# Gate weights split ahead of their stage, w2's last units in other buffers, and a second plain block at the start of FFN-b

## The chip, the cores and the metric

The kernel runs on one core of one Trainium2 chip. The metric is device microseconds of one execution. Its engines are called here by the profile's names: PE is TensorE (PEld its weight loads), DVE is VectorE, ACT is ScalarE, POOL is GpSimd, SP is SyncE, which issues nearly all transfers of this kernel.

## What is computed

One layer of a decoder trunk, for 1024 prompt rows and 32 sample rows that share the weights. They are handled together as 1056 columns.

```python
def swiglu(x, w1, w3, w2):
    return (jax.nn.silu(x @ w1) * (x @ w3)) @ w2

h = layer_norm(ALPHA * x + 0.5 * swiglu(x, f1_w1, f1_w3, f1_w2), ln1_g, ln1_b)      # FFN-a
z = h @ w_in + b_in                       # q, k, v, the gMLP's u and v, and two gates ga, gb
# att: dilated sliding-window attention on q, k, v;  yb: gMLP branch on u, v
mix = (jax.nn.sigmoid(ga) * (att @ w_oa) + jax.nn.sigmoid(gb) * (yb @ w_ob)) @ w_out
h = layer_norm(ALPHA * h + mix, ln2_g, ln2_b)
h = layer_norm(ALPHA * h + 0.5 * swiglu(h, f2_w1, f2_w3, f2_w2), ln3_g, ln3_b)      # FFN-b
```

D_MODEL is 1024, D_FF is 2816, so the hidden layer of an FFN is 22 blocks of 128 rows. All data is fp32.

## The kernel before

**Tiles.** Features lie on the 128 partitions, the 1056 columns in four chunks c = 0 to 3 of C = 264. Every fp32 operand is split into a high part (a cast to fp32r on ACT) and a low part (a subtraction on DVE), line 237, and every product is three matmuls of 128x128 by 128x264 (`mm3`, line 223): high by high, high by low, low by high. All of them carry line 227 in the profile.

**FFN** (`ffn`, line 641, called with i = 0 for FFN-a and i = 2 for FFN-b). The 22 hidden blocks are worked in two ways:

- `hidden8` (407) is the plain way: per chunk 8 x 3 matmuls for w3 and as many for w1, then Silu on ACT and a product on DVE. Block 0 is done so, chunk by chunk, while the chunks of the input become ready.
- `hidden` (424) is one level of Strassen over pairs of chunks and halves of the features: seven products of 2 x 4 x 3 matmuls each. `prep` (355) makes the sums of weights for it, a step per product of the block before; on DVE for the first two blocks, then on POOL. Its first two products need only chunks 0 and 2. `spread` (314) makes the sums of the input.

Blocks 0, 19, 20 and 21 (`PLAIN`) go as hidden rows to DRAM; the other 18, in pairs, go there as the sums that w2's Strassen needs (`spill_sums`, 459).

**The w2 stage** (`out`, 785). Three groups g of four blocks np run `seven` (762), with the sums loaded from DRAM ahead. In the last group `plain_sums` (798) reads the four plain blocks' hidden rows, splits them and writes both parts to DRAM (`parted`). In the last block, `fetch` loads them back (H, two slots each), and `units2` (757) loads w2's four units for the plain blocks, through a raw buffer each and a split. Then, per chunk, eight `block(n, c)` add the plain blocks' product, a unit for two n; two of the four units are taken in chunk 0, at n = 1 and 3 (line 898). `center` (518) subtracts the mean, with two DVE subtractions one step apart (line 537), `square_step` sums squares, and `norm` (582) makes the LayerNorm of a chunk: sums by PE (589), inverse root (`rsqrt`, 628: Sqrt on ACT, then four DVE operations), broadcast by PE (597), scaling on DVE (608) and ACT (616), and a split. Each chunk's LayerNorm runs beside the next work.

**After FFN-a** (`widen`, 1047): six of the sixteen gate blocks are multiplied the plain way (`gate8`, 948), the first three chunk by chunk while the LayerNorm ends, then three more (1077); then the Strassen pairs of w_in. Their weights are loaded by `unit` (212): a raw buffer, a cast, a subtraction. The first three are taken during w2's chunk 2 (line 892). The attention and the rest of the layer follow (`mix`, 1488). It ends with w_out and LayerNorm 2, whose last chunks overlap block 0 of FFN-b (673 to 683); block 0's weights are loaded at line 1626.

**Order and buffers.** The program order is what the code below writes; a scheduler then places each instruction by priority and by its own timeline, within each engine's order. `high_priority` moves a piece ahead; `fenced` and `chained` keep background pieces behind what was marked. Background work is written as generators in the queues `bg`, `slow` and `mid`, each stepped a few times after a product (`tick`, 179; the counts are in `STEPS`). `tables` (908) is such a piece, in FFN-a's w2 stage. On-chip buffers are taken from pools by tag: 37 slots S, 8 W, 2 raw R, 2 Q, 6 M. A transfer or an instruction that needs a buffer waits until one is free. `copy_state` (205) attaches pieces of a copy of state, DRAM to DRAM, to the loads of weights.

Of the kernel before, what the change touches and what calls it, by code (L numbers as in the profile page):

```python
# [13 lines left out]
F32R = mybir.dt.float32r  # L14
AF = mybir.ActivationFunctionType
# [49 lines left out]
WARM = 2  # L65
FENCED = (mybir.EngineType.DVE, mybir.EngineType.Activation, mybir.EngineType.SP)
# [5 lines left out]
EARLY = 6  # L72
CHUNKED = 3
# [6 lines left out]
class Trunk:  # L80
# [131 lines left out]
    def unit(self, src, n=D, slot=False, ahead=URGENT):  # L212
        new = self.S if slot else self.W
        with self.tc.high_priority(offset=ahead):
            raw = self.R([P, D])
            hi, lo = new([P, D], F32R), new([P, D], F32R)
            dma = self.nc.sync.dma_start(raw[:, :n], src[:, :n])
            self.split(hi[:, :n], lo[:, :n], raw[:, :n])
        self.fence[mybir.EngineType.SP] = dma.ins
        self.copy_state(dma, 1)  # L220
        return hi, lo
# [296 lines left out]
    def center(self, c, hs, rest, m=None, parts=1):  # L518
        nc = self.nc
        start = 0 if m is None else KB // 2 - 1  # L520
        t = self.M([P, C])
        y = self.Y[c]
        tt = nc.vector.tensor_tensor
        for i in range(start, KB // 2):
            m = self.gather(c, i, m)
            yield
        tt(t, m[:, 0], m[:, 1], op=ALU.add)
        tt(t, t, hs[:, c * C : c * C + C], op=ALU.add)
        yield from self.pause(rest)
        pm = self.ax_tile()[:, :C]  # L530
        nc.tensor.matmul(pm, self.ones, t, start=True, stop=True)
        yield from self.pause(rest if parts == 1 else 2)
        q = KH // parts
        for j in range(2):
            for x in range(0, KH, q):
                e = y[j][:, x : x + q]
                tt(e, e, pm.unsqueeze(1).to_broadcast([P, q, C]), op=ALU.subtract)
            yield
# [43 lines left out]
    def norm(self, c, i, mode, Y, s):  # L582
# [7 lines left out]
        r, t = self.X([P, 3], "rs"), self.X([P, 3], "rt")  # L590
        self.rsqrt(r, t, pv, EPL)
# [35 lines left out]

    def rsqrt(self, r, t, v, eps):
        tt = self.nc.vector.scalar_tensor_tensor
        self.nc.scalar.activation(r, v, AF.Sqrt, bias=self.eps[eps])  # L630
        self.nc.vector.reciprocal(r, r)
        tt(t, v, eps, r, op0=ALU.add, op1=ALU.mult)
        tt(t, t, -0.5, r, op0=ALU.mult, op1=ALU.mult)
        self.chain = tt(r, t, 1.5, r, op0=ALU.add, op1=ALU.mult).ins
# [6 lines left out]
    def ffn(self, w13, w2p, w2, i, mode, resid):  # L641
        nc, preps = self.nc, {}
        last = FB + NG * (KB // 2) - 1
# [27 lines left out]
        else:  # L671
# [17 lines left out]
        def ready(f):  # L689
            for _ in preps.pop(f):  # L690
                pass
            if f < last:
                begin(f + 1)

        def between(f, bg, slow=0):
            if f + 1 in preps:
                next(preps[f + 1], None)
            self.tick(bg, slow)
# [7 lines left out]
        for f in range(1, FB):  # L706
# [5 lines left out]
            def after():  # L712
# [4 lines left out]
            self.hidden(f, after)  # L717
            del self.L[f]
# [66 lines left out]
    def out(self, w2, i, mode, ready, between, load):  # L785
        nc = self.nc
        f = FB
        self.w2units, self.spare = self.units2(w2), False
# [4 lines left out]
        def fetch(k):  # L793

            if k < NPL:
                H.append(self.load_hidden(k))

# [33 lines left out]
        for g in range(NG):  # L831
            for np in range(KB // 2):
                final = g == NG - 1 and np == KB // 2 - 1
                if g == NG - 2 and np == 0:
# [9 lines left out]
                ready(f)  # L844

                def step(p):
# [26 lines left out]
        self.spare = True  # L873
# [13 lines left out]
        for c in range(NC):  # L887
            early = 6 if c == 0 else 0
            if mode != "out":
                self.hold_normed(c)  # L890
                if c == 2:
                    self.early = [self.unit(self.a["wzp"][n], slot=True, ahead=AFTER) for n in range(CHUNKED)]
            for n in range(KB):
# [4 lines left out]
                if c == 0 and n in (1, 3):  # L898
                    W2.append(next(self.w2units))
# [147 lines left out]
    def widen(self):  # L1047
# [585 lines left out]
    def run(self):  # L1633
# [8 lines left out]
        self.parted = parted("A")  # L1642
        self.ffn(a["w13a"], a["w2pa"], a["w2a"], 0, "spill", a["xc"])
# [150 lines left out]
```

## Time and profile before

| what | us |
|---|---|
| median of 3 runs | 2209.47 |
| lowest, highest | 2204.01, 2209.97 |
| the profiled execution's own time | 2205.9 |
| its span, first to last instruction | 2204.1 |

How to read the profile's lines. A line of a group or of the order of time names the engine, the line of the kernel, the operation, what it writes <- what it reads (buffer numbers left out), shapes, and xcount; in the order of time it begins with the start and the duration in us, and the bracket at its end is the idle time of the engine just before it and who ended it. SPq marks the issue of a transfer. A line of stretches is A:B and its length, then busy us and (xcount) of PE, PEld, DVE, ACT and POOL, the granted TensorE clock as a share of full speed, the mean busy share of the 16 DMA engines and GB/s. A line of one tile's operations gives the least, median and greatest duration in ns, first and last start in us, and the forms.

### The profile page before, as it was taken

The numbers are of one execution on the slowest core, as the hardware profiler recorded it, in microseconds if no ns is written. First come the engines' busy times: TensorE is split into PE (matmuls) and PEld (weight loads), VectorE is DVE, ScalarE is ACT, GpSimd is POOL, SyncE is SP. The second block draws the span as 40 slices with busy tenths as digits, with TensorE's granted clock in tenths as the row PEclk, the third lists the DMA queues.
The fourth block names the chain that finished last, engine by engine and source line by source line (L and its number), as shares of the span: only waits on it lengthen the run. The fifth ranks groups of instructions, "written<-read, shape, count | busy, mean of one in ns | idle before, by whom it ended". The sixth has DMA issues, their size and how long they took to land.

```text
span 2204.1 us, 43247 instructions
## 1 busy us (share of the span) xinstructions
PE 2148.7 (97%) x17281; PEld 2097.4 (95%) x17281; DVE 1560.7 (71%) x2718; ACT 899.0 (41%) x1690; POOL 327.2 (15%) x238
## 2 busy tenths in 40 slices
PE   9999999999999999999889998998999999999997
PEld 8999999999999999999878888998999999999997
DVE  8777777656788636888574648878676676657787
ACT  5444444421226634344365444246444444422224
POOL 0432332100010021322000000000432332100000
PEclk9999999999999999999989999999999999999999
DMA  4445545598874325666844647513445545597752
GB/s 157 146 142 178 169 160 190 182 381 315 337 269 145 121 102 190 222 213 243 289 155 147 186 133 236 202 44 132 165 156 176 175 160 181 186 381 268 294 191 79
DMA packets 170553, 429.82 MB, mean 195 GB/s; under 512 B 24864, under 2 KB 61456, under 8 KB 167664
## 3 DMA queue, kind: packets, MB, share of 16 engines
q1 hardware_dynamic: 169920, 426.53, 55.1%
q8 instruction: 135, 2.21, 0.4%
q10 hardware_dynamic: 432, 0.54, 0.1%
q14 instruction: 66, 0.54, 0.1%
HBM read 305.97 MB, written 167.22 MB: 215 GB/s over the span
## 4 chain that ended last, share of the span: by engine, by line
PE 84%; DMA 6%; DVE 6%; ACT 1%; issue 1%; POOL 1%; SPq 0%; ACTq 0%; DVEq 0%; POOLq 0%
PE ax L227 44%; PE mm L227 35%; DMA M<-kv 3%; PE ax L1164 1%; DVE W L239 1%; DMA R<-wz 1%; PE ax L1187 1%; PE ax L1203 1%; DMA S<-zD 1%; DVE S L239 1%; DVE S L608 1%; DMA S<-cD 0%; DMA R<-w2a 0%; DVE X L1346 0%; DVE M L1356 0%
## 5 line engine op out<-in xcount | busy, mean ns | idle before, releaser
L227 PE MATMUL ax<-S,W 128*128 128x264 f32 x5472 | 716.2, 285 | 0.8 <-ACT S L994 0.5
L227 PE MATMUL mm<-S,W 128*128 128x264 f32 x5040 | 676.8, 289 | 21.8 <-DVE S L1505 8.6
L227 PEld LDWEIGHTS ax<-S,W 128*128 128x128 f32 x5472 | 685.6, 188 | 3.4 <-ACT S L994 1.5
L227 PEld LDWEIGHTS mm<-S,W 128*128 128x128 f32 x5040 | 639.2, 190 | 37.9 <-DVE S L1505 8.9
L227 PE MATMUL ax<-S,S 128*128 128x264 f32 x3288 | 483.6, 285 | 3.1 <-DVE S L1003 3.0
L227 PEld LDWEIGHTS ax<-S,S 128*128 128x128 f32 x3288 | 434.1, 188 | 4.2 <-DVE S L1003 4.1
L227 PE MATMUL mm<-S,S 128*128 128x264 f32 x2496 | 390.3, 287 | 9.0 <-ACT S L238 4.5
L227 PEld LDWEIGHTS mm<-S,S 128*128 128x128 f32 x2496 | 339.8, 190 | 11.6 <-ACT S L238 4.9
L238 ACT CAST W<-R 128x256 fp32r<-128x256 f32 (+2 forms) x172 | 127.6, 759 | 323.6 <-PE mm L227 128.6
L369 POOL TENSOR_TENSOR Q<-R 128x512 f32<-128x512 f32 x50 | 70.7, 1415 | 793.9 <-DMA R<-w13b 240.2
L239 DVE TENSOR_TENSOR W<-R,W 128x256 fp32r<-128x256 f32 (+2 forms) x172 | 149.2, 872 | 27.1 <-ACT W L238 26.8
L238 ACT CAST W<-Q 128x1024 fp32r<-128x1024 f32 (+1 forms) x79 | 77.8, 985 | 216.5 <-POOL Q L370 89.8
L780 DVE SCALAR_TENSOR_TENSOR S<-ax,S 128x264 f32<-128x264 f32 x240 | 100.0, 432 | 69.1 <-PE ax L227 67.8
L444 DVE TENSOR_TENSOR S<-ax,M 128x264 f32<-128x264 f32 x84 | 33.7, 433 | 157.5 <-PE ax L227 157.5
L106 POOL CAST S<-ones 128x1 fp32r<-128x1 f32 x32 | 17.6, 571 | 752.5 <-DVE S L1583 366.5
L239 DVE TENSOR_TENSOR S<-Q,S 128x1024 fp32r<-128x1024 f32 (+1 forms) x79 | 114.0, 1443 | 3.4 <-ACT S L238 3.3
L239 DVE TENSOR_TENSOR W<-Q,W 128x1024 fp32r<-128x1024 f32 (+1 forms) x79 | 91.9, 1163 | 24.7 <-ACT W L238 24.7
L238 ACT CAST S<-Q 128x1024 fp32r<-128x1024 f32 (+1 forms) x79 | 77.8, 984 | 73.7 <-PE ax L227 54.6
L238 ACT CAST S<-R 128x512 fp32r<-128x512 f32 (+1 forms) x65 | 44.6, 686 | 110.7 <-DMA sumsA<-S 35.7
L239 DVE TENSOR_TENSOR S<-S,M 128x528 fp32r<-128x528 f32 x72 | 84.0, 1166 | 3.5 <-ACT M L238 1.9
L370 POOL TENSOR_TENSOR Q<-Q,R 128x512 f32<-128x512 f32 x50 | 83.4, 1668 | 2.7
L377 POOL TENSOR_TENSOR Q<-R,Q 128x512 f32<-128x512 f32 x50 | 81.7, 1634 | 1.2
(199 smaller groups left out, 2095.8 us busy)
## 6 DMA issues: line engine op xcount, KB each, us to landing
ws<-st SPq DMA_DIRECT2D x144, 256.0 KB
S<-sumsA SPq DMA_DIRECT2D x63, 528.0 KB
S<-sumsB SPq DMA_DIRECT2D x63, 528.0 KB
M<-kv SPq DMA_DIRECT2D x96, 256.0 KB
sumsA<-M SPq DMA_DIRECT2D x90, 264.0 KB
sumsB<-M SPq DMA_DIRECT2D x90, 264.0 KB
R<-w13b SPq DMA_DIRECT2D x44, 512.0 KB
S<-zD SPq DMA_DIRECT2D x42, 528.0 KB
```

The lines of the kernel that those rows point to most:

```text
L227: mm = lambda a, b, s, e: nc.tensor.matmul(o, a[:, cc], b, start=s, stop=e, skip_group_check=True)
L238: a = self.nc.scalar.copy(hi, src)
L239: b = self.nc.vector.tensor_tensor(lo, src, hi.bitcast(F32), op=ALU.subtract)
L369: tt(s12[:, lo], cd[:, lo], cd[:, hi], op=ALU.add)
L370: tt(s12[:, hi], s12[:, lo], ab[:, lo], op=ALU.subtract)
L377: tt(s34[:, hi], ab[:, hi], s12[:, hi], op=ALU.subtract)
L444: go(one, 5, False, lambda x: tt(h[:, x, 1], one[x], p7[:, x], op=ALU.add))
L608: nc.vector.tensor_tensor(y, y, pb.unsqueeze(1).to_broadcast([P, KH, C]), op=ALU.mult)
L780: nc.vector.scalar_tensor_tensor(y(x, r, e), bank[x], HALF, y(x, r, e), op0=ALU.mult, op1=ALU.add)
L1164: nc.tensor.matmul(pS[h][:, r, :nk], q[e, i * P : (i + 1) * P], k[e, k0 : k0 + nk], start=True, stop=True)
L1187: nc.tensor.transpose(pT[r][:, h, o], s[:, r, h, o], self.ident)
L1203: nc.tensor.matmul(pv[0][e, (i % 4) * P : (i % 4 + 1) * P], V[:, i - (nb - 1) + b, e], sT[:, r, h, b * P : b * P + P], start=b == 0, stop= ...
```

## The change

1. **Gates.** A new background piece, `part_gates`, starts with FFN-a's w2 stage. It loads the six gate blocks' weights in twelve halves, splits them and writes both parts to DRAM. `gate_unit` later loads the two parts straight into S slots (the first three) or W (the rest), where `unit` loaded one raw block and split it. In `widen`, the first Strassen pair's preparation is fenced and chained.
2. **w2's units, both FFNs.** All four are taken in the last block of the w2 stage, in an order with the fetches given by `FINAL` (0 is a unit, k is a fetch). Units three and four use the raw buffers Q, not R. No state copy is attached to them.
3. **Center.** In the w2 stage the two subtractions of chunks 1 to 3 are three steps apart, not one.
4. **FFN-b** begins with two plain blocks, 0 and 19, chunk by chunk in turn; block 19's Strassen form is dropped. The input's second `spread` enters the background before the last chunk.
5. **Inverse root on DVE** (`rsqrt_dve`): eleven DVE operations from a bit pattern and three Newton steps, in LayerNorm 2's last chunk and the last LayerNorm's chunk 2. After LayerNorm 2's chunk 2, ACT runs a small Silu.

```diff
+MAGIC = float(0x5F3759DF)
+FINAL = ((1, 0, 0), (0,), (2, 0), (3,))
...
-    def unit(self, src, n=D, slot=False, ahead=URGENT):
+    def unit(self, src, n=D, slot=False, ahead=URGENT, raw=None, copies=1):
...
-            raw = self.R([P, D])
+            raw = (raw or self.R)([P, D])
...
+    def part_gates(self):
+        nc = self.nc
+        halves = [(n, slice(e, e + D // 2)) for n in range(NLEAD) for e in (0, D // 2)]
+        raws = deque()
+
+        def start():
+            if todo:
+                n, e = todo.popleft()
+                raws.append(self.M([P, D // 2]))
+                nc.sync.dma_start(raws[-1], self.a["wzp"][n][:, e])
+
+        todo = deque(halves)
+        start()
+        yield from self.pause(3)
+        for n, e in halves:
+            start()
+            yield
+            raw = raws.popleft()
+            hi = self.M([P, D // 2], F32R)
+            self.split(hi, raw.bitcast(F32R), raw)
+            nc.sync.dma_start(self.gates[n][0][:, e], hi.bitcast(F32))
+            nc.sync.dma_start(self.gates[n][1][:, e], raw)
+            yield
+
+    def gate_unit(self, n, slot=False):
+        new = self.S if slot else self.W
+        with self.fenced():
+            t = [new([P, D], F32R) for _ in range(2)]
+            for x, src in zip(t, self.gates[n]):
+                dma = self.nc.sync.dma_start(x.bitcast(F32), src)
+        self.fence[mybir.EngineType.SP] = dma.ins
         self.copy_state(dma, 1)
...
-            yield
+            yield from self.pause(1 if m is None or parts > 1 else MID)
...
+        if c == NC - 1 and i == 1 or c == NC - 2 and mode == "out":
+            self.rsqrt_dve(r, t, self.X([P, 3], "rx", 1), pv, EPL)
+        else:
+            self.rsqrt(r, t, pv, EPL)
+        if i == 1 and c == NC - 2:
+            nc.scalar.activation(self.X([P, 2], "warm", 1)[:, :1], r[:, :1], AF.Silu)
...
+    def rsqrt_dve(self, r, t, x, v, eps):
+        nc = self.nc
+        tt = nc.vector.scalar_tensor_tensor
+        nc.vector.tensor_scalar(x, v, eps, None, op0=ALU.add)
+        nc.vector.tensor_scalar(r.bitcast(I32), x.bitcast(I32), -0.5, MAGIC, op0=ALU.mult, op1=ALU.add)
+        for _ in range(3):
+            nc.vector.tensor_tensor(t, x, r, op=ALU.mult)
+            tt(t, t, -0.5, r, op0=ALU.mult, op1=ALU.mult)
+            self.chain = tt(r, t, 1.5, r, op0=ALU.add, op1=ALU.mult).ins
...
+        plain = PLAIN[: 1 if i == 0 else 2]
+        blocks = [f for f in range(FB) if f not in plain] + [FB + g for g in range(NG * (KB // 2))]
...
+            lead = [units] + [[self.unit(w13[f, x]) for x in range(2)] for f in plain[1:]]
             begin(1)
             for c in range(NC):
                 self.drain(lns.pop(c))
-                self.hidden8(units, 0, c)
-                if c:
-                    with self.chained():
-                        next(preps[1], None)
-            self.bg.append(s1)
+                if c == NC - 1:
+                    self.bg.append(s1)
+                    self.step(self.bg, 2)
+                for f, u in zip(plain, lead):
+                    self.hidden8(u, f, c)
+                    if c:
+                        with self.chained():
+                            next(preps[1], None)
...
-            yield self.unit(w2[u * n : u * n + n].rearrange("(p x) -> p x", p=P), D, self.spare)
+            yield self.unit(w2[u * n : u * n + n].rearrange("(p x) -> p x", p=P), D, u > 1, raw=self.Q if u > 1 else self.R, copies=0)
...
+        def last(j):
+            for k in FINAL[j]:
+                if k:
+                    fetch(k)
+                else:
+                    W2.append(next(self.w2units))
...
+                if g == 0 and np == 0 and mode != "out":
+                    self.bg.append(self.part_gates())
...
+                if final:
+                    last(0)
...
-                    if final:
-                        fetch(k + 1)
-                        if k in (4, 6):
-                            W2.append(next(self.w2units))
+                    if final and k < len(FINAL) - 1:
+                        last(k + 1)
...
-                    self.early = [self.unit(self.a["wzp"][n], slot=True, ahead=AFTER) for n in range(CHUNKED)]
+                    self.early = [self.gate_unit(n, True) for n in range(CHUNKED)]
...
-                if c == 0 and n in (1, 3):
-                    W2.append(next(self.w2units))
...
         for n in range(CHUNKED, NLEAD):
-            w = self.unit(a["wzp"][n])
+            w = self.gate_unit(n)
             if n == NLEAD - 1:
-                begin(0)
+                with self.fenced():
+                    begin(0)
             for c in (1, 3, 0, 2):
                 self.gate8(w, DENSE[n], c, AF.Sigmoid, STEPS["lead"], 1)
                 if n == NLEAD - 1:
-                    next(preps[0], None)
+                    with self.chained():
+                        next(preps[0], None)
...
+        self.gates = [[dram(f"gate{n}{j}", [P, D]) for j in range(2)] for n in range(NLEAD)]
```

More of the change, by code (lines that the diff above doesn't have):

```diff
@@ L14 @@
 F32R = mybir.dt.float32r
+I32 = mybir.dt.int32
 AF = mybir.ActivationFunctionType
@@ L642, in ffn @@
         nc, preps = self.nc, {}
-        last = FB + NG * (KB // 2) - 1
+        plain = PLAIN[: 1 if i == 0 else 2]
+        blocks = [f for f in range(FB) if f not in plain] + [FB + g for g in range(NG * (KB // 2))]
+        after = dict(zip(blocks, blocks[1:]))
         def begin(f):
@@ L691, in ready @@
                 pass
-            if f < last:
-                begin(f + 1)
+            if f in after:
+                begin(after[f])
         def between(f, bg, slow=0):
-            if f + 1 in preps:
-                next(preps[f + 1], None)
+            if after.get(f) in preps:
+                next(preps[after[f]], None)
             self.tick(bg, slow)
@@ L704, in load @@
                     loads.popleft()()
-        for f in range(1, FB):
+        for f in blocks[: FB - len(plain)]:
             ready(f)
@@ L710, in ffn, with step @@
             count = iter(range(1, 8))
-            def after():
+            def step():
                 between(f, STEPS["strassen"])
@@ L715, in after @@
                     load(min(HEAD, 2 + 4 * next(count)))
-            self.hidden(f, after)
+            self.hidden(f, step)
             del self.L[f]
@@ L787, in out @@
         f = FB
[L788 removed]
+        self.w2units = self.units2(w2)
         sums = self.column_sums(w2, NPL)
```

10 lines of the change are left out of this document (6 added, 4 removed).

## The prediction, as it went on record

> **What bounds the kernel now.** I read the page first, then the busy time by stretches of 25 us, then the order of time around each stretch in which TensorE falls behind, then the waits.
>
> ```profile
> span 2204.1 us, 43247 instructions
> PE 2148.7 (97%) x17281; PEld 2097.4 (95%) x17281; DVE 1560.7 (71%) x2718; ACT 899.0 (41%) x1690; POOL 327.2 (15%) x238
> ```
>
> TensorE is busy 97% of the span; no other engine is over 71% (VectorE, DVE). A change that leaves its matmuls alone can win only its holes: 2204.1 - 2148.7 = 55 us, plus stretches that count as busy at a slow clock. The stretches show where they are.
>
> ```profile
> 650.00:675.00 25.00, 21.75 (x157) 20.77 (x155) 18.53 (x33) 6.41 (x11) 1.25 (x6) 0.93 0.73 271
> 1500.00:1525.00 25.00, 20.59 (x146) 19.87 (x145) 21.45 (x31) 14.49 (x19) 0.00 (x0) 0.86 0.40 135
> 1600.00:1625.00 25.00, 25.00 (x208) 25.00 (x207) 18.28 (x26) 10.75 (x19) 5.66 (x4) 1.00 0.45 149
> ```
>
> The last row is the measure: 208 matmuls in 25 us, 0.120 us each. The other two, at the end of FFN-a and the start of FFN-b, hold 157 and 146, the second at a clock of 0.86. The change touches both places, and adds work in FFN-a's w2 stage (about 471 to 656 us).
>
> **End of FFN-a (w2's last units, gates split ahead, center spread).** In order of time:
>
> ```profile
> 640.41 0.81 SPq L217 DMA_DIRECT2D R<-w2a  x2
> 649.72 0.34 SPq L217 DMA_DIRECT2D R<-w2a  x1
> 659.92 1.05 ACT L238 CAST S<-R 128x1024 fp32r<-128x1024 f32 x1 [13.38 <-DMA R<-w2a]
> 661.02 0.75 PE L227 MATMUL mm<-S,S 128*128 128x264 f32 x4 [0.49 <-ACT S L238]
> 662.41 1.22 DVE L239 TENSOR_TENSOR S<-R,S 128x1024 fp32r<-128x1024 f32 x1
> 663.69 5.68 PE L227 MATMUL mm<-S,S 128*128 128x264 f32 x32 [1.92 <-DVE S L239]
> 664.00:668.00 4.00, 4.00 (x24) 4.00 (x23) 2.76 (x5) 0.94 (x2) 0.00 (x0) 0.62 0.76 241
> 672.85 2.41 DVE L537 TENSOR_TENSOR S<-S,ax 128x1056 f32<-128x1056 f32 x2
> 676.62 3.19 PE L227 MATMUL mm<-S,W 128*128 128x264 f32 x24 [2.43 <-DVE S L885]
> ```
>
> The third w2 unit is late: the two R buffers were taken by units one and two, so its load could be issued only some 9 us after theirs. TensorE waits 0.49 + 1.92 us, and its next 32 matmuls take 5.68 us where 32 x 0.120 = 3.84 would do (granted clock 0.62): 1.84 more. Then two center subtractions back to back (2.41 us) hold up the PSUM eviction: 2.43. Together 6.7 us. With units three and four in Q and SBUF slots, and three yields between the two subtractions, all of it can go.
>
> The Trainium skill, "TensorE: Matmul & The Clock Gate", Part 1 (What's actually happening), says that the clock halves only after an idle window of about 3.4 us; by it the 1.84 would not belong to these waits and the sum would be 4.8. The rows show a drop after 2.4 us of waiting within 3.2, so I keep 1.84.
>
> What is late next is the load of H, the plain blocks' hidden rows:
>
> ```profile
> S<-partA SPq DMA_DIRECT2D x8, 528.0 KB
> R<-w2a SPq DMA_DIRECT2D x4, 512.0 KB
> 655.21 1.51 PE L227 MATMUL mm<-S,W 128*128 128x264 f32 x11
> 575.00:612.00 37.00, 36.75 (x301) 36.53 (x301) 27.33 (x60) 8.86 (x15) 0.00 (x0) 1.00 1.03 402
> ```
>
> All 12 transfers now stand before the first plain matmul at 655.2, the last pair of H behind all four w2 units: 8 x 0.541 + 4 x 0.524 = 6.4 MB, at the 402 GB/s of the saturated stretch 16 us from 640.4, so 656.4, against a need at about 655.2 + 9 x 0.120 = 656.3. It just fits; I allow 1 us (0, if S slots let them start earlier, to 4, with a slow clock behind). **Term: -5.7, between -6.7 and -2.4** (only the subtraction's hole goes). The gate units come from DRAM already split: six casts and six subtractions like 659.92 and 662.41 (1.05 on ACT, 1.22 on DVE) leave the stretch up to 745. Neither bounded TensorE beyond what is counted, so zero more. Their 12 loads for 6 are issued a chunk (96 matmuls) and more before use. The state copy that each w2 unit carried moves behind later loads, and no engine waits for copies: zero. The new fences in `widen` keep an order in a stretch without TensorE waits: zero.
>
> **The price in FFN-a's w2 stage.** `part_gates` issues 12 loads and 24 stores of 256 KB, 12 casts and 12 subtractions of 512 columns. The engines' rows for the same work on 528 columns are `plain_sums`' eight halves, which run in this stage already:
>
> ```profile
> L238 ACT CAST M<-M x8: 627/632/637, 574.6 to 626.9; 128x528 fp32r<-128x528 f32 x8
> L239 DVE TENSOR_TENSOR M<-M,M x8: 698/704/717, 598.8 to 633.8; 128x528 fp32r<-128x528 f32 x8
> PE ax L227 <- DVE W L239: 0.3, 1, 0.3
> 450.00:495.00 45.00, 45.00 (x372) 45.00 (x371) 24.03 (x53) 9.56 (x18) 0.00 (x0) 1.00 1.03 399
> 495.00:515.00 20.00, 20.00 (x164) 19.70 (x164) 16.42 (x37) 3.85 (x6) 0.00 (x0) 1.00 0.51 169
> 515.00:570.00 55.00, 55.00 (x431) 51.93 (x429) 38.38 (x84) 8.50 (x14) 0.00 (x0) 1.00 0.97 364
> ```
>
> So 12 x 0.63 = 7.6 us of ACT and 12 x 0.70 = 8.4 of DVE, spread over some 14 products; DVE is busy 24 of 45 and 16.4 of 20 us there, and an eviction delayed by 0.7 us has another PSUM pair to hide behind. The transfers are the question. 36 x 0.262 = 9.4 MB at 402 GB/s are 23.5 us of all 16 engines, in a stage in which they are full for 450 to 495 and nearly for 515 to 570; the hole 495 to 515 has 0.49 x 20 = 9.8 us. So up to 13.7 us of transfers is pushed into the next full stretch, together with whatever stands behind them in SP's one queue: the sums of the next group and the w2 blocks' own loads. How near those are:
>
> ```profile
> 537.06 0.33 SPq L361 DMA_DIRECT2D R<-w2pa  x1
> 543.56 1.51 ACT L238 CAST W<-R 128x768 fp32r<-128x768 f32 x3 [11.80 <-DMA R<-w2pa]
> 548.85 0.95 DVE L239 TENSOR_TENSOR W<-R,W 128x768 fp32r<-128x768 f32 x1
> ```
>
> The load lands 6.5 us after issue and its split ends on DVE some 5 us later, in its tick's turn: about 4 us of slack. For nothing lost speaks that `plain_sums` does the same (8 loads, 16 stores) inside 575 to 612, full at 1.03, and TensorE waits 0.3 us in the whole stage; against it, that this is 50% more of it, and that the M buffers are shared with `tables`, which may spread it further. **Term: +1.5, between 0 and 10.** The skill's "DMA: Bandwidth & Descriptors" (Where 436 GB/s comes from) puts the HBM limit of a core at about 358 GB/s, by which the transfers would take 26.4 us; the row of 402 stands.
>
> **Start of FFN-b (two plain blocks, inverse root on DVE).**
>
> ```profile
> 1487.42 8.89 PE L227 MATMUL mm<-S,S 128*128 128x264 f32 x72
> 1496.49 1.28 ACT L415 ACT_TABLE_LOAD   x1
> 1498.22 2.81 PE L227 MATMUL mm<-S,S 128*128 128x264 f32 x21 [1.91 <-ACT M L415]
> 1505.38 3.20 PE L227 MATMUL mm<-S,S 128*128 128x264 f32 x24 [0.38 <-ACT M L415]
> 1515.01 1.07 ACT L238 CAST S<-S 128x1056 fp32r<-128x1056 f32 x1
> 1516.13 0.81 PE L227 MATMUL mm<-S,S 128*128 128x264 f32 x2 [3.97 <-ACT S L238]
> 1519.64 6.78 PE L227 MATMUL mm<-S,S 128*128 128x264 f32 x46
> 1526.90 1.73 PE L227 MATMUL mm<-S,W 128*128 128x264 f32 x12 [0.48 <-ACT M L415]
> ```
>
> Block 0 begins at 1487.42, chunk by chunk. It waits 1.91 and 0.38 us for Silu behind table loads, and 3.97 for the last chunk's LayerNorm; then 60 matmuls (2, 12 hoisted, 46) take 1516.13 to 1526.42, 10.3 us for 7.2: 3.1 more, slow clock and the wait for the low half. With 0.48 at the end: 9.8 us. Now chunks 0 to 2 give 3 x 96 matmuls of cover: 1487.4 + 288 x 0.120 = 1522, past the 1516.1 and the 1519.6 at which the chunk's halves were ready, and the chain is shorter. Its root takes 11 small DVE operations; two such in a row, and block 1's first load as it is now:
>
> ```profile
> 1482.40 0.16 DVE L632 SCALAR_TENSOR_TENSOR X<-ax,X 128x3 f32<-128x3 f32 x1
> 1482.59 0.16 DVE L633 SCALAR_TENSOR_TENSOR X<-X,X 128x3 f32<-128x3 f32 x1
> 1485.64 0.33 SPq L361 DMA_DIRECT2D R<-w13b  x1
> 1489.15 1.06 ACT L238 CAST W<-R 128x1024 fp32r<-128x1024 f32 x1 [3.40 <-DMA R<-w13b]
> ```
>
> 0.2 us apart, so 2.2 us, and no table load between root and Silu. The price is certain: a plain block is 8 x 3 x 2 x 4 = 192 matmuls, the Strassen block it replaces 7 x 24 = 168; 24 x 0.120 = +2.9. Uncertain is block 19's weights: their loads take R where block 1's first load was (1485.64, landed by 1489.15, the second some 1.1 us later), and their subtractions meet a DVE busy 21 of 25 us, with need at 1487.4 + 5.8 = 1493.2. I take +1, between 0 and 5. DVE's own sum (two splits 2.4, four products 1.7, root +1.4) is 5.5 us, and the stage gets 384 x 0.120 + 1.4 = 47.5 us where it had 39.5. **Term: -9.8 + 2.9 + 1 = -5.9, between -6.9 and -1.9.**
>
> **The tail.**
>
> ```profile
> 2168.68 1.71 PE L227 MATMUL mm<-S,W 128*128 128x264 f32 x12 [1.25 <-DVE S L885]
> ```
>
> 1.25 us are a subtraction pair again and should go. Chunk 2's root on DVE adds 7 operations, 7 x 0.2 = 1.4 us, to DVE just ahead of the last chunk's chain, which nothing covers, and takes the ScalarE hop out of chunk 2's; between none and all of the 1.4 I take the middle. **Term: -0.5, between -1.3 and +1.4.**
>
> **Sum.** -5.7 + 1.5 - 5.9 - 0.5 = -10.6 us, against the profiled execution's own 2205.9: 2195.3. The median shown, 2209.47, lies 3.6 above that execution, the lowest 1.9 below; I forecast 2196.
>
> **Rivals.**
> 1. The transfers bound the w2 stage (slower). Place: 500 to 560 us, SP's queue behind the gates' stores. Price: the 13.7 us pushed past the hole, paid once by TensorE, plus about 2 us of slow clock after each of three waits: 20, so -12.1 + 20 = +8, 2214. It makes the kernel slower by 0.3% once the stage loses 12.1 + 6.6 = 18.7 us. For it: the full rows and 4 us of slack. Against: `plain_sums` cost nothing. Chance 0.14.
> 2. The same in part, some 6 to 8 us: 2201. Chance 0.08.
> 3. Block 19's weights and DVE's backlog eat the start of FFN-b: term 0 for -5.9, 2201. Chance 0.10.
> 4. The change doesn't do what it says at w2's last units: they find no slots before the products free them, and TensorE waits there as before; -2.4 for -5.7, 2198.6. Chance 0.08.
>
> **How the numbers follow.** The forecast has 0.60. Its own bounds reach from -6.7 - 6.9 - 1.3 = -14.9 (2191) to about 2200; with the runs' scatter below, 2188. Upwards the range takes in cases 2 to 4 and the median's height, 2208; case 1 stays out. 0.3%, 6.6 us, is about what a measurement of this kernel can tell from no change. Faster: 0.60 + 0.08 = 0.68; within: cases 2 and 3, 0.18; slower: 0.14.
>
> **What would show it.** Right: no TensorE wait over 0.5 us between 655 and 680 and a granted clock of 1.00 there; w2's last two loads issued before 650; no table load between chunk 2's root and block 1 of FFN-b, and the last chunk begun without a wait. Wrong: TensorE waits on a w2 block's split or on the sums between 490 and 570, with DMA shares at 1.03 through 495 to 515; or a wait at block 19's first chunk.

## The result, and the profile after

The changed kernel takes 2218.21 us (median of 10 runs, 2214.4 to 2225.7), the kernel before 2209.6 beside it: a ratio of 1.0049, between 1.0036 and 1.0061. It is slower, by 8.6 us between the medians; 2196 was forecast.

The page's first lines. TensorE is as busy as before, in a longer span:

```profile
span 2217.9 us, 43388 instructions
PE 2153.4 (97%) x17305; PEld 2100.4 (95%) x17305; DVE 1554.9 (70%) x2730; ACT 893.8 (40%) x1687; POOL 319.0 (14%) x234
```

So the place has to be found by stages. The bounds of each are the start of a line's first or last instruction: the PSUM evictions of w2's Strassen blocks, the gates' first and last Sigmoid, w_out's last eviction, the first eviction of w2's plain blocks in FFN-b. Both kernels were profiled twice (the second time as e12 and e11 below).

| stage, us | before, twice | after, twice | first to first | forecast |
|---|---|---|---|---|
| FFN-a's w2 stage (Strassen) | 190.96, 190.87 | 215.18, 215.13 | +24.2 | +1.5 (0 to 10) |
| FFN-a's end, plain blocks to first gate | 61.18, 62.58 | 51.76, 51.77 | -9.4 | -5.7 (-6.7 to -2.4) |
| the six gates | 72.98, 72.98 | 71.85, 71.85 | -1.1 | 0 |
| w_in's pairs, attention, w_out | 700.56, 707.50 | 706.71, 702.30 | +6.2 | 0 |
| FFN-b to w2's plain blocks | 649.27, 649.08 | 643.39, 643.48 | -5.9 | -5.9 |
| tail | 64.71, 64.69 | 64.72, 64.73 | 0.0 | -0.5 |

The attention differs by 6.9 us between two executions of the *same* kernel before, and by 4.4 between two of the changed one, so its +6.2 shows no effect of the change. Every other row repeats within 1.4 us, those of the changed kernel within 0.1.

The rows don't hold the same matmuls before and after. FFN-a's end holds 22 fewer and the six gates 9 fewer: 7 of them were pulled ahead into the w2 stage, and 24 now stand behind the last gate, in the attention's row. At 0.12 us each that is all of the gates' -1.1, and 2.9 of the +6.2. Without the attention the rows sum to +7.8; with these 2.9 it is +10.7, against 8.6 between the medians and an attention that scatters by 7. One term went wrong by more than that: the w2 stage.

The stretches of after that answer to those of before (columns as explained above):

```profile
495.00:515.00 20.00, 20.00 (x166) 20.00 (x165) 14.58 (x32) 5.21 (x10) 0.00 (x0) 1.00 0.82 304
515.00:570.00 55.00, 40.06 (x256) 34.29 (x254) 29.63 (x59) 10.91 (x18) 0.00 (x0) 0.81 0.89 336
```

Until 515 nothing is lost (166 matmuls in 20 us). Then 256 matmuls stand where 431 stood, at a clock of 0.81. The waits of TensorE in after (460 to 690 us), with total, times and longest in us:

```profile
PE mm L264 <- DMA S<-sumsA: 10.8, 2, 8.5
PE ax L264 <- DVE S L840: 3.2, 5, 1.6
...
```

Five more of 0.4 to 0.7 each make 16.6 us in all, and the two long ones are for the sums of w2's next group. In order of time:

```profile
527.29 0.63 PE L264 MATMUL mm<-S,S 128*128 128x264 f32 x3 [2.33 <-DMA S<-sumsA]
536.41 1.00 PE L264 MATMUL mm<-S,W 128*128 128x264 f32 x3 [8.49 <-DMA S<-sumsA]
```

After them the clock is down. Two stretches of after, and the same 35 us of before and after:

```profile
527.00:537.00 10.00, 1.22 (x6) 1.04 (x6) 2.49 (x5) 0.00 (x0) 0.00 (x0) 0.55 0.95 383
537.00:545.00 8.00, 7.63 (x21) 3.49 (x21) 1.56 (x3) 0.62 (x1) 0.00 (x0) 0.50 0.46 140
515.00:550.00 35.00, 23.31 (x129) 18.58 (x128) 15.64 (x32) 5.84 (x10) 0.00 (x0) 0.71 0.87 334
```
```profile
515.00:550.00 35.00, 35.00 (x273) 32.92 (x272) 21.16 (x45) 5.38 (x9) 0.00 (x0) 1.00 1.02 403
```

Before's row has 35.00 / 273 = 0.128 us for a matmul; 129 of them are 16.5 us, and TensorE was busy for 23.3: 6.8 us of slow clock. 16.6 + 6.8 = 23.4. The stage holds 7 matmuls more than before, 0.8 us: 24.2, the whole of the row.

Why were the sums late? The larger transfers issued from 507 to 529 us, in before and then in after:

```profile
S<-sumsA SPq DMA_DIRECT2D x14, 528.0 KB
R<-w2pa SPq DMA_DIRECT2D x2, 384.0 KB
ws<-st SPq DMA_DIRECT2D x2, 256.0 KB
```
```profile
S<-sumsA SPq DMA_DIRECT2D x12, 528.0 KB
R<-w2pa SPq DMA_DIRECT2D x4, 384.0 KB
gate<-M SPq DMA_DIRECT2D x4, 256.0 KB
ws<-st SPq DMA_DIRECT2D x3, 256.0 KB
M<-wzp SPq DMA_DIRECT2D x2, 256.0 KB
```

Issued are 8.9 MB before and 10.4 MB after; at 402 GB/s that is 22 and 26 us of all engines, in 22 us. Before just fitted, with 14 loads of sums; after holds 12 and is over. The order of SP's queue in after shows the sums between the gates' transfers:

```profile
520.76 0.33 SPq L235 DMA_DIRECT2D M<-wzp  x1
522.37 0.32 SPq L798 DMA_DIRECT2D S<-sumsA  x1
524.06 0.32 SPq L247 DMA_DIRECT2D gate<-M  x1
...
526.00 2.30 SPq L798 DMA_DIRECT2D S<-sumsA  x3
```

The 24th load of sums in this stage was issued at 527.31 before and at 540.21 after: by then each wait of TensorE also holds the slots that the next sums need (SP waits 5.2 us for one).

### The profile page after: what moved, and what is told of

Its sections match the earlier page's. It is cut to its first block, busy times and chain, and to the rows that moved or that the text cites. A ratio compares the mean times of both kernels' runs of the same rounds, so it can differ in the third digit from the quotient of the medians.

```text
span 2217.9 us, 43388 instructions
## 1 busy us (share of the span) xinstructions
PE 2153.4 (97%) x17305; PEld 2100.4 (95%) x17305; DVE 1554.9 (70%) x2730; ACT 893.8 (40%) x1687; POOL 319.0 (14%) x234
## 4 chain that ended last, share of the span: by engine, by line
PE 81%; DMA 9%; DVE 6%; issue 1%; POOL 1%; ACT 1%; SPq 1%; ACTq 0%; DVEq 0%; POOLq 0%
PE ax L264 42%; PE mm L264 35%; DMA M<-kv 3%; PE ax L1232 1%; DMA R<-wz 1%; DVE W L276 1%; PE ax L1255 1%; PE ax L1271 1%; DMA S<-zD 1%; DMA S<-w2a 1%; DMA R<-w2pa 1%; DMA gate<-M 0%; DMA S<-cD 0%; DVE X L1414 0%; DVE M L1413 0%
## 5 line engine op out<-in xcount | busy, mean ns | idle before, releaser
L264 PE MATMUL mm<-S,W 128*128 128x264 f32 x5208 | 699.5, 289 | 31.8 <-DVE S L1573 10.3
L264 PE MATMUL ax<-S,W 128*128 128x264 f32 x5400 | 706.7, 285 | 3.9 <-DVE S L840 2.3
L264 PEld LDWEIGHTS mm<-S,W 128*128 128x128 f32 x5208 | 660.7, 191 | 46.5 <-issue 16.8
L264 PEld LDWEIGHTS ax<-S,W 128*128 128x128 f32 x5400 | 677.0, 188 | 8.0 <-DVE S L840 3.3
L264 PE MATMUL mm<-S,S 128*128 128x264 f32 x2472 | 383.3, 285 | 3.5 <-DMA S<-sumsA 2.3
L264 PEld LDWEIGHTS mm<-S,S 128*128 128x128 f32 x2472 | 333.6, 188 | 4.7 <-DMA S<-sumsA 2.5
L275 ACT CAST W<-R 128x1024 fp32r<-128x1024 f32 (+3 forms) x170 | 126.1, 756 | 280.8 <-PE mm L264 124.3
L276 DVE TENSOR_TENSOR W<-R,W 128x1024 fp32r<-128x1024 f32 (+3 forms) x170 | 146.4, 866 | 35.2 <-ACT W L275 35.0
L275 ACT CAST M<-M 128x528 fp32r<-128x528 f32 (+1 forms) x82 | 51.4, 627 | 91.8 <-DMA gate<-M 22.8
L276 DVE TENSOR_TENSOR M<-M,M 128x528 fp32r<-128x528 f32 (+1 forms) x82 | 74.9, 913 | 9.8 <-ACT M L275 9.8
```

What stands on the lines that cost most here:

```text
L264: mm = lambda a, b, s, e: nc.tensor.matmul(o, a[:, cc], b, start=s, stop=e, skip_group_check=True)
L275: a = self.nc.scalar.copy(hi, src)
L276: b = self.nc.vector.tensor_tensor(lo, src, hi.bitcast(F32), op=ALU.subtract)
```

## The experiments

**Theory.** The 36 transfers overfill a stage whose 16 DMA engines were full; sums come late, TensorE waits, its clock falls. **Rivals.** The order in SP's queue, not the bytes; the M buffers, shared with `tables` and `plain_sums`; the splits' turn on the in-order ACT and DVE; or parts 2 to 5.

Every kernel differs from the changed one by its edit, of which the lines that matter are shown. Where the gates' two parts aren't made or aren't used, the gates are loaded by `unit` as before. The stage's lengths are those of the table above (before: 191.0 and 61.2; after: 215.2 and 51.8).

| run | w2 stage, us | FFN-a's end, us | median, us | ratio to before, 95% |
|---|---|---|---|---|
| e1 no part 1 | 192.8 | 59.3 | 2205.77 | 0.9989 (0.9977 to 1.0002) |
| e2 gates in Strassen stage, in M | 193.0 | 52.6 | 2206.81 | 0.9994 (0.9981 to 1.0007) |
| e3 an eighth of the columns | 200.6 | 58.9 | 2207.52 | 0.9995 (0.9986 to 1.0005) |
| e4 tables later | 217.6 | 50.5 | 2216.49 | 1.0037 (1.002 to 1.0055) |
| e5 transfers alone | 201.5 | 59.7 | 2212.89 | 1.0025 (1.0016 to 1.0034) |
| e6 stores from POOL | 217.5 | 51.9 | 2221.4 | 1.0065 (1.0049 to 1.0081) |
| e7 three gates | 201.3 | 53.0 | 2205.7 | 0.9987 (0.9978 to 0.9997) |
| e8 parts 3 to 5 alone | 190.9 | 62.6 | 2202.63 | 0.9974 (0.9963 to 0.9984) |
| e9 three gates in Strassen stage, in S | 192.8 | 58.7 | 2199.95 | 0.9968 (0.9956 to 0.9981) |
| e10 six gates in Strassen stage, in S | 192.8 | 52.6 | 2199.13 | 0.9964 (0.9952 to 0.9976) |
| e13 gates in w2 stage, in S | 211.6 | 52.9 | 2217.38 | 1.0039 (1.0025 to 1.0053) |

**e1, part 1 undone.** `gate_unit` becomes `unit` again, the fences in `widen` go, and

```diff
-                if g == 0 and np == 0 and mode != "out":
-                    self.bg.append(self.part_gates())
```

> The changed kernel without its part 1: no part_gates, the gate weights loaded raw and split as before, the fences of the first Strassen pair's preparation taken out; parts 2 to 5 stay. Theory A (the gates' transfers and buffers cost the w2 stage of FFN-a, everything else gains as forecast): the w2 stage takes the 191 us of before again, from first to last eviction of the seven products, where the changed kernel takes 215; time about 2220.7 - 24 = 2197, some us more because the gate splits come back beside LayerNorm 1; ratio to before about 0.995. Theory B (another part of the change, or the new order that the scheduler makes, costs it): the stage stays over 200 us or the time over 2206.

The stage's loss is gone (+1.8, with 6 matmuls pulled ahead in it), so it belongs to part 1. The time, 2205.8, isn't the 2197 of Theory A, since little of the gain elsewhere is left. FFN-a's end gains only 1.9, and holds 24 matmuls less than before, 2.9 us: net nothing. TensorE's waits there (650 to 735 us) say why:

```profile
PE mm L264 <- DMA S<-partA: 3.8, 3, 2.9
PE mm L264 <- DVE S L951: 3.0, 3, 1.7
```

The issues of e1 ahead of the plain blocks, H in two halves:

```profile
643.25 1.68 SPq L220 DMA_DIRECT2D Q<-w2a  x2
648.00 0.33 SPq L220 DMA_DIRECT2D R<-wzp  x1
649.75 0.33 SPq L220 DMA_DIRECT2D R<-wzp  x1
650.74 4.03 SPq L787 DMA_DIRECT2D S<-partA  x4
```

Two gate loads stand ahead of H's second half. In the changed kernel the gates' loads come some 13 us behind H's, and nothing of H is waited for (below).

**e2, the same gates begun in FFN-a's Strassen stage**, ahead of block 4, in place of their start in the w2 stage; still in M.

```diff
+            if i == 0 and f == 4:
+                self.bg.append(self.part_gates())
```

> part_gates starts at FFN-a's block 4 of the Strassen stage, where the DMA engines are about half busy, in place of the w2 stage; all else as in the changed kernel. Theory A1 (it is the full DMA engines of the w2 stage): the w2 stage is back at about 191 us and the Strassen stage hides 9.4 MB, about 23 us of transfers in some 50 us; time 2195 to 2198. Theory A2 (it is the shared M buffers, or SP's queue standing still behind the gates' stores, wherever they are): waits of several us appear among the Strassen blocks, which hold three M buffers themselves; time over 2203.

The w2 stage is near e1's and FFN-a's end gains 8.6, but the Strassen stage loses 9.6. Its waits (50 to 470 us):

```profile
PE ax L264 <- ACT M L477: 6.0, 2, 4.3
```

It is the copy of a block's first product into a buffer M (L477); this stage takes three M for each block, and more for the sums of each pair. The 24 matmuls behind the longest of these waits took 5.53 us, 2.6 more than 24 x 0.12. Moving the work is right; M is the wrong buffer there.

**e3, an eighth of the columns, unused.** The loads and stores take the same slice as the split.

```diff
+            x = slice(0, 64)
...
-            self.split(hi, raw.bitcast(F32R), raw)
+            self.split(hi[:, x], raw.bitcast(F32R)[:, x], raw[:, x])
...
```

> part_gates stays in the w2 stage with all its instructions, buffers, waits and 36 transfers, but each transfer and each split takes 64 of 512 columns; what it writes is not used, and the gate weights are loaded raw and split as before. Theory A1 (bytes): the w2 stage loses under 3 us against before's 191; time about that of the kernel without part 1. Theory A2 (buffers, queue order, waits for casts): the stage still loses 15 us or more; time over 2210.

+9.6 us in the stage, between the two expectations: the bytes are not all of the price. The splits are short here too (a cast 0.25 us for 0.62, a subtraction 0.22 for 0.69), so what is left is the price of the instructions' turn, the buffers and the queue, more than of busy engines. TensorE's waits (515 to 660 us) are for evictions on DVE and, at a matmul of `tables`, one that is put down to a load of w2's weights:

```profile
PE ax L265 <- DVE S L841: 4.2, 6, 1.1
PE ax L1011 <- DMA R<-w2pa: 2.2, 1, 2.2
```

**e4, `tables` two blocks later** (`np == 1` to `np == 3`).

> The changed kernel with the piece tables started two blocks later (at the fourth block of the first group, not the second), so that part_gates has the M buffers alone while it runs; bytes and their place are the same. Theory A1 (bytes in a full stretch): the w2 stage still loses 12 us or more against 191, with TensorE waiting for the sums of group two; time over 2208. Theory A2 (M buffers shared with tables): part_gates ends some 14 products after it starts, the stage loses under 6 us; time under 2204.

It moves the waits and not the price: +26.6. Theory A1 expected waits for the sums, and there are none. The longest wait (440 to 700 us) is that of a matmul of `tables`, for loads that SP issued from 568.6 us, behind the last of the gates' stores:

```profile
PE ax L988 <- DMA M<-ohP: 7.4, 1, 7.4
```

So `tables` and `part_gates` still collide in this run, and it can't acquit `tables`. e13 does so better: TensorE doesn't wait at a matmul of `tables` there, and the stage still loses 20.6.

**e5, the transfers alone, no split.**

```diff
-            hi = self.M([P, D // 2], F32R)
-            self.split(hi, raw.bitcast(F32R), raw)
-            nc.sync.dma_start(self.gates[n][0][:, e], hi.bitcast(F32))
+            nc.sync.dma_start(self.gates[n][0][:, e], raw)
...
```

> The changed kernel with part_gates reduced to its transfers: 12 loads, and each half is stored twice as it came, so that no cast, no subtraction and no second M buffer belong to it; the 36 transfers keep their size and place. What is stored isn't used (it isn't split), the gates are loaded and split by unit as before, and parts 2 to 5 stay. The stage of w2 in FFN-a took 24.1 us longer than before in the changed kernel, 1.8 with no part_gates at all, and 9.9 with 64 of the 512 columns. Theory (bytes and SP's one queue): the bytes were 14 of the 24, so this keeps 14 to 20 of it, and the kernel comes to 2216 to 2222. Rival (buffers M and the splits' turn on ACT and DVE): without them the stage loses under 6 us and the kernel comes to 2205 to 2211.

+10.5: between the two expectations. Against e1, which has neither, all bytes without splits cost 8.7 (e5), all instructions with an eighth of the columns 7.8 (e3), and the whole 22.4: two parts of like size, and 6 us more than their sum. The bytes alone don't make the sums late: e5 waits for none, but (515 to 660 us) 4.4 us for splits of w2's own weights, with the slow clock behind.

**e6, the 24 stores from POOL's queue.**

```diff
-            nc.sync.dma_start(self.gates[n][0][:, e], hi.bitcast(F32))
+            nc.gpsimd.dma_start(self.gates[n][0][:, e], hi.bitcast(F32))
...
```

> The changed kernel with the 24 stores of part_gates issued from POOL's queue, so that they don't stand before the loads of the sums and of w2's weights in SP's queue; bytes, buffers and splits are the same. Theory A (the order in SP's queue): the wait for the sums of 2 and 8.5 us at 524 to 536 goes, the stage loses 8 to 14 us instead of 24, and the kernel comes to 2204 to 2211. Theory B (the DMA engines are full, whoever issues): the stage loses 20 us or more and the kernel stays at 2214 to 2220. POOL's own sums of weights wait behind stores that wait for a split; that could give a new wait of TensorE on W.

Theory B: +26.5 (the time, 2221.4, is 1.4 above its range), and the sums are waited for as in the changed kernel (515 to 660 us):

```profile
PE mm L264 <- DMA S<-sumsA: 11.1, 4, 7.9
```

The stores' place in SP's queue isn't the cause. The 12 loads stayed in that queue; no run moves them. The Trainium skill, "DMA: Bandwidth & Descriptors" (Issuing engines are not separate DMA queues), says that transfers issued by different engines run on the same 16 DMA engines and interleave; this run agrees (a stage of 217.5 us, 215.2 with the stores in SP's queue).

**e7, three gates ahead of time instead of six.**

```diff
-        halves = [(n, slice(e, e + D // 2)) for n in range(NLEAD) for e in (0, D // 2)]
+        halves = [(n, slice(e, e + D // 2)) for n in range(CHUNKED) for e in (0, D // 2)]
```

> The changed kernel with three gate blocks split ahead, not six (the three that widen takes early); the other three are loaded and split by unit as before. 18 transfers of 256 KB are 4.7 MB, 11.7 us of 16 engines at 402 GB/s, against 9.8 us of free engine time in the stage before. Theory (bytes beyond the free engine time are what is paid): the stage loses 3 to 9 us, not 24; FFN-a's end keeps most of its gain of 9.4 us, since the early three are the ones whose splits lay there, and the kernel comes to 2199 to 2206. Rival (each piece costs by its structure, buffers and queue): half of 24, and the kernel comes to 2207 to 2212.

The stage loses 10.3 for half the transfers and nearly all of FFN-a's end is won. The theory put the stage at 3 to 9, since it counted the hole of 495 to 515 as free; the time, 2205.7, fell within its range. Its waits for the sums were 2.6 us (3 of them, 2.0 the longest), yet:

```profile
527.00:537.00 10.00, 8.95 (x35) 6.84 (x33) 6.65 (x14) 2.81 (x5) 0.00 (x0) 0.51 1.00 369
```

35 matmuls at a clock of 0.51: 35 x 0.128 = 4.5 us of work took 8.95, so the slow clock costs more than the waits did.

**e8, parts 3 to 5 alone** (part 1 undone as in e1, w2's units as in the kernel before).

> The kernel before with parts 3, 4 and 5 alone: no part_gates, gates loaded and split by unit, w2's units taken as before. In the changed kernel the start of FFN-b gained 7.3 us, with part 1 undone 6.0, and with part 1 undone FFN-a's end gained only 1.9, since TensorE waited there 3.8 us for hidden rows that now stand behind four units. Theory (the parts add): w2's stage as before, FFN-a's end -2 to -4 (the subtraction's hole of 2.43), the start of FFN-b -6, the tail 0 to +1.5: 2199 to 2203, faster than the kernel with part 1 undone. Rival (what is won ahead is lost in the attention and after it, as the 1.9 to 6 us between the gate pairs and w_out in the other runs): 2205 to 2208.

Faster, by the start of FFN-b. FFN-a's end, expected at -2 to -4, gains nothing: the pair of subtractions (L574) still runs back to back, behind a gate's subtraction, and still holds TensorE.

```profile
672.20 1.23 DVE L276 TENSOR_TENSOR S<-R,S 128x1024 fp32r<-128x1024 f32 x1 [1.23 <-ACT S L275]
673.34 2.41 DVE L574 TENSOR_TENSOR S<-S,ax 128x1056 f32<-128x1056 f32 x2
676.77 4.72 PE L264 MATMUL mm<-S,W 128*128 128x264 f32 x24 [2.91 <-DVE S L952]
```

**e9 and e10, the gates in FFN-a's Strassen stage and in S slots**, three or six, one after each second or fourth block:

```diff
+            if i == 0 and f in (4, 6, 8, 10, 12, 14):
+                g = self.part_gate((4, 6, 8, 10, 12, 14).index(f))
+                with self.fenced():
+                    next(g)
+                self.bg.append(g)
```

`part_gate` loads a whole block into an S slot; its split and two stores are the generator's second step.

> Three gate blocks split ahead, but in FFN-a's Strassen stage, where the 16 DMA engines are 35 to 59% busy (50 to 425 us), and in S slots, not in M: a load after blocks 4, 8 and 12, its split and two stores queued behind that block's sums. Nothing of it is left in the stage of w2. Parts 2 to 5 stay. Theory (the price of splitting ahead is the full engines and the shared M buffers of the stage of w2, not the work itself): the Strassen stage and the stage of w2 take within 1.5 us of before (with three gates in the w2 stage it lost 9.2), FFN-a's end keeps 8 of gain, the start of FFN-b 6, and the kernel comes to 2194 to 2199. Rival (the work costs wherever it is put: DVE and ACT are in order, and S slots are short): 5 to 9 us lost in the Strassen stage, and 2201 to 2206 as with three gates in the w2 stage.

> The same with all six gate blocks: loads after blocks 4, 6, 8, 10, 12 and 14, used by gate_unit as in the changed kernel. With all six and M buffers, begun at block 4 in one piece, the Strassen stage lost 9.6 us to two waits for Silu's buffer M, and the kernel came to 2206.8. Theory: spread out and in S slots that goes, the kernel comes to 2193 to 2200, and the rest between the gates and w_out shows whether six blocks from DRAM cost there (6 to 11 us more than before in three of the four runs that used six, 2 at most in those that used none or three). Rival: S slots are short, DVE is 70% busy, and the Strassen stage loses 5 us or more: 2203 to 2209.

Both beat both kernels. The w2 stage is e1's; the Strassen stage loses 1.1 us with three and 3.6 with six. e9's end of FFN-a, where 8 us of gain were expected, gains 2.5: it has e1's wait for H (2.9 the longest), with two of `unit`'s gate loads again ahead of H's second half. (e7 has them there too and doesn't wait; its w2 stage is 8 us longer.) e10 has nearly all of the gain of FFN-a's end. It came to 2199.1, within what was expected; e9 came to 2200.0, 1 above it.

**e11 and e12, the changed kernel and the one before, profiled again.**

> The changed kernel, profiled once more: how much of each stage's time is the kernel's own and how much differs from execution to execution. Theory: the stage of w2 in FFN-a is again 20 us or more longer than before, with TensorE waiting for the sums. If the 6 us between the gates' lead and w_out that the changed kernel lost in its first profile come back, they belong to the kernel; if they move by several us, they belong to the execution.

> The kernel before, profiled once more, for the same purpose: the stages of the first profile should come back within 1 us each if the schedule alone sets them; differences of 2 us and more in the attention would say that the small drifts seen there in the other runs are scatter.

The w2 stage repeats within 0.1 us, the attention does not within 6. But for the 24 matmuls more that stand there in each kernel with six gates ahead, the attention's differences in the other runs are therefore left unexplained.

**e13, `part_gates` where it is, in S slots** (`self.M` to `self.S` for both tiles).

> The changed kernel, part_gates at its place in FFN-a's w2 stage with its 36 transfers and its splits, but its halves lie in S slots instead of M; nothing else is different. The stage lost 24.1 us (23.9 when profiled again): 16.8 of waits and about 8 of slow clock. Theory A (the shared M buffers are the second half of the price: with an eighth of the bytes 9.9 were lost, with the transfers alone 11.0): with M free, tables and the splits go at their old pace, about 9 to 13 us of the stage's loss remain, those of the bytes, and the kernel comes to 2201 to 2209. Theory B (bytes and the splits' turn on DVE and ACT, whatever the buffer, or S slots that the sums need): 20 us or more remain, and 2213 to 2222.

+20.6: Theory B. Taking the halves out of M doesn't take the second half of the price away; that the S slots, which the sums need too, took its place isn't excluded. The waits (464 to 700 us) now begin with casts of w2's own weights that come late on ACT:

```profile
PE mm L264 <- ACT S L275: 3.9, 1, 3.9
PE ax L264 <- ACT W L275: 2.8, 2, 1.9
```

One measure beside another, 515 to 612 us: before, after, e5 and e10.

```profile
515.00:612.00 97.00, 96.75 (x766) 92.85 (x765) 70.02 (x153) 19.45 (x31) 0.00 (x0) 1.00 0.95 364
```
```profile
515.00:612.00 97.00, 80.23 (x574) 73.19 (x573) 60.92 (x132) 18.11 (x30) 0.00 (x0) 0.89 0.91 335
```
```profile
515.00:612.00 97.00, 92.62 (x703) 87.80 (x702) 67.10 (x147) 17.35 (x30) 0.00 (x0) 0.96 1.00 374
```
```profile
515.00:612.00 97.00, 96.75 (x765) 92.57 (x765) 69.66 (x154) 18.11 (x29) 0.00 (x0) 1.00 0.95 360
```

766 matmuls become 574 in after and 765 in e10; 192 x 0.126 = 24.2 us. e5's 703 stand for 8 us.

## Why the prediction was wrong

**FFN-a's w2 stage: the step that failed.** The term was +1.5 with a bound of 10. It measured +24.2, or 23.4 without the 7 matmuls: 16.6 us of waits and 6.8 of slow clock. The step that failed is the overlap: the transfers that don't fit the hole, priced at 13.7 us of all engines, were taken as nearly all covered. The ground for it, that `plain_sums` does the same, was no evidence: that its 24 transfers are covered shows nothing of 36 more in another stretch. The bound of 10 left out the slow clock, and the price of the splits beyond their busy time (e3: 9.6 us with an eighth of the columns).

A second sentence is wrong as well. "The hole 495 to 515 has 0.49 x 20 = 9.8 us" took idle engines for free ones. In before the engines were idle there because SP, which issues in order, stood still: from 491.5 to 501.9 at a load of the next block's weights, and from 504.7 to 510.4 at the first load of the next group's sums. Its waits in before, 490 to 512 us (total, times, longest), were for a Q buffer and for an S slot:

```profile
SPq L361 <- DVE Q L377: 10.4, 1, 10.4
SPq L738 <- PE ax L227: 6.3, 3, 5.7
```

What is queued behind such a load can't use the hole while it waits, and the burst of sums comes after it in any case. In after SP still waits 5.6 us for Q there; the share rose from 0.51 to 0.82, so 0.31 x 20 = 6.2 of the 9.8 us were used. The 3.6 us that were not are the smaller part of the miss.

Rival 1 named this place and this mechanism and priced it at 20. It was wrong in one thing: that the sums stand behind the gates' stores in SP's queue doesn't matter (e6). What is shown is the place: with `part_gates` out of this stage, the loss is gone (e1, e2, e9, e10). It has not been shown that the bytes by themselves hold back the sums: e5, with all of them, loses 8.7 us without a wait for sums. Nor is it settled how the rest divides between the order on ACT and DVE, the buffers, the 12 loads in SP's queue and `tables`. In after, from 515 to 590, ACT stood 18.4 us at casts of `part_gates` until a store had left their M buffer; whether TensorE paid for that, no run shows, and e13 shows only that the price stays when the halves leave M.

**FFN-a's end** was -9.4, forecast -5.7. It holds 22 matmuls fewer, 2.6 us, so -6.8 net: just past the bound of -6.7. That it came near is luck, since the reason was wrong. I gave the gain to parts 2 and 3 and "zero more" to the gates that come split. e1 (parts 2 and 3, no split gates) and e8 (part 3 alone) gain nothing net; with the early gates split each run gains 8 us or more, as long as H isn't late. Part 3 doesn't part the two subtractions in time: in after they still run back to back, and TensorE isn't held.

```profile
691.38 2.41 DVE L574 TENSOR_TENSOR S<-S,ax 128x1056 f32<-128x1056 f32 x2
```

What is gone is the gate's subtraction right ahead of them, in before:

```profile
671.71 1.23 DVE L239 TENSOR_TENSOR S<-R,S 128x1024 fp32r<-128x1024 f32 x1 [0.62 <-ACT S L238]
```

From e1 to e10 TensorE's waits of 650 to 735 us fall from 3.8 us for H and 3.0 for evictions to 1.0 and 0.3, 5.5 of the 6.7 us between their rows. So it is the gates' subtractions on DVE, and their loads ahead of H, whose absence counts. Nor is the 1.84 of slow clock sure: in e12 the same waits (0.44 + 1.97) were followed by the same 32 matmuls in 4.18 us.

That H's loads "just fit" wasn't put to the test in after, whose last Strassen eviction came 19.2 us behind w2's first load, for 15.0 in before. The issues and the one wait left (675 to 735 us):

```profile
660.29 0.81 SPq L220 DMA_DIRECT2D R<-w2a  x2
661.19 1.88 SPq L787 DMA_DIRECT2D S<-partA  x4
663.16 1.44 SPq L220 DMA_DIRECT2D Q<-w2a  x2
664.69 3.52 SPq L787 DMA_DIRECT2D S<-partA  x4
```
```profile
PE mm L264 <- DVE S L953: 0.3, 1, 0.3
```

In e10, with 16.8 us, H is waited for 1.0 us, the 1 that I allowed.

**FFN-b** was right: -5.9 for -5.9, though the match to the tenth is luck, since the other runs with this start have -4.5 to -6.1. The one wait left at its start is block 19's weights, 1.41 us where I allowed 1; no chunk waits for LayerNorm, and the root takes 1524.54 to 1526.87, 2.3 us for my 2.2.

```profile
1514.89 4.17 PE L264 MATMUL mm<-S,W 128*128 128x264 f32 x32 [1.41 <-DVE W L276]
```

**The tail** was 0.0 for -0.5. The 1.25 fell to 0.3, though the pair runs back to back here too. Chunk 2's root on DVE now holds TensorE for 1.64 us, where before it waited 0.98 for the last chunk's squares, and the last chunk's own wait grew by 0.4. Before, and then after:

```profile
2194.56 1.42 PE L597 MATMUL ax<-ident,X 128*128 128x128 f32 x6 [2.27 <-DVE X L634]
```
```profile
2204.49 0.81 PE L640 MATMUL ax<-ident,X 128*128 128x128 f32 x6 [1.64 <-DVE X L679]
2208.65 1.42 PE L640 MATMUL ax<-ident,X 128*128 128x128 f32 x6 [2.69 <-DVE X L687]
```

With the first part moved and every other kept, the kernel comes near the forecast: e10 measures 2199.1, 3 above 2196.

## What to carry to other kernels

A dip in the DMA engines' share isn't all spare room when the queue that feeds them stands still: look at who holds that queue before transfers are put there, and add up the bytes that are issued in the burst behind it. Work that is to be done ahead of time goes where engines, buffers and transfers all have room (here a stage with shares of 0.35 to 0.59 and free S slots), not where the code happens to be near. Count a transfer that comes late twice: the wait, and the slow clock behind it.

## What the runs showed of the hardware

- The clock fell without a long wait. In e7 four waits of 0.26, 0.33, 2.04 and 0.27 us within 5 us were followed by 10 us at 0.51 (527 to 537). The Trainium skill, "TensorE: Matmul & The Clock Gate", Part 1 (What's actually happening), puts the half clock behind an idle window of about 3.4 us. After's wait of 8.49 us agrees with that; e7 doesn't, since none of its waits is near it. Nor does the same wait always cost the same: before's 0.49 + 1.92 us were followed by 4 us at 0.62 (664 to 668), and in e12, the same kernel, 0.44 + 1.97 by 4 us at 1.00.
- One core alone moved 396 to 416 GB/s in stretches of 8 to 45 us, for loads and stores together (399 in before, 450 to 495; 396 in after, 515 to 527; 416 in e13, 537 to 545).
- The same kernel's attention took 700.6 us in one execution and 707.5 in another, while every stage around it repeated within 1.4 us. What differs there wasn't looked into.
